# A convolutional feed-forward up-projection: 40 of 44 pairs of feature blocks as seven half-width products each, with activations parked in DRAM until the down-projection

## The chip, the cores and the metric

One NeuronCore of one Trainium2 chip runs the whole layer as one program. The metric is the device time of an execution in microseconds (us). All matmuls take float32r operands; each float32 matrix is split into a rounded part `hi` and a remainder `lo`, and a product is three matmuls (hi·hi, hi·lo, lo·hi).

## The reference

One encoder layer on 512 positions of width 2048: latent attention beside a gated convolution, an output projection, and then the part that the change touches:

```python
h = rmsnorm(x, ffn_norm_g[l])
u = conv3_centred(h @ w_ffn_up[l], ffn_conv_w[l]) + ffn_conv_b[l]   # (512, 2*5632)
g, val = u[..., :D_FF], u[..., D_FF:]
x = x + (jax.nn.silu(g) * val) @ w_ffn_down[l]                       # 5632 -> 2048
return rmsnorm(x, final_norm_g)
```

## The kernel before

Everything is kept transposed: a tile is 128 features (partitions) by 512 positions. Weights come from DRAM as units of 128x1024 (eight 128x128 blocks, 512 KB, array `wall`). For each unit SP issues the load into a `raw` tile (3 buffers), ScalarE casts it to `hi` (line 214), VectorE subtracts to get `lo` (line 211), and TensorE runs 24 matmuls of 512 columns on it (lines 224 and 227 to 231). `hi` and `lo` have two buffers, so the split of a unit can begin when TensorE has finished the unit two before.

`items` is the list of TensorE's work, one entry per unit. `run` walks it: it keeps two units split ahead and three loaded ahead, and calls each item's follow-up functions (`posts`) a given number of items later. A scheduler then sets each engine's final order by its own model of time; each engine runs its queue strictly in order.

A **block** below is one value of `f` (0 to 43): 128 gate features and the 128 value features that belong to them. `up(f)` makes four units of it (two per side, 16 blocks of the contraction over 2048): 96 matmuls of 512 columns. `conv` multiplies the sum in PSUM by the norm factor `rx.r` on VectorE, applies the middle tap and bias on ScalarE (line 465), the two outer taps on VectorE (lines 466 and 467), and silu on the gate side (line 761). `gate` multiplies the sides and splits the result into the pair `acts[f]`, which stays in SBUF. `down(c, f0)` follows after a chunk of eight blocks: 16 units that read the eight pairs and add into the residual tiles `xr` (line 211, `l<-ps,l`). Up and down work therefore alternate by chunk. The last chunk of four goes through `last_half` in two halves of 256 positions (matmuls of 256 columns), followed by the final norm and the stores.

`h2` holds the 16 scaled and split residual tiles, the moving operand of every up-projection matmul. PSUM has eight banks of 128x512.

Of the kernel before, what the change touches and what calls it, by code (L numbers as in the profile page):

```python
# [32 lines left out]
P = 128  # L34
# [17 lines left out]
NT = 76  # L52
# [43 lines left out]
def pack_weights(w_in, w_q_b, w_kv_b, w_o, w_up, w_down):  # L96
# [12 lines left out]
    for i, u in enumerate(UNITS):  # L109
# [24 lines left out]
        elif k == "up":  # L134
            c = u[1] * FF + u[2] * P
            wall[i] = kblock(w_up, 8 * u[3], 8, slice(c, c + P))
# [9 lines left out]
class Item:  # L146
# [3 lines left out]
    def __init__(self, pe, key=None, part=slice(0, UW), posts=()):  # L150
        self.pe, self.key, self.part, self.posts = pe, key, part, list(posts)
# [3 lines left out]
def encoder_block(ctx: ExitStack, tc: tile.TileContext, gx, wall, vecs, rot, out):  # L155
# [3 lines left out]
    lp = ctx.enter_context(tc.tile_pool(name="lp", bufs=KD))  # L159
    xp = ctx.enter_context(tc.tile_pool(name="xp", bufs=2))  # L160
# [14 lines left out]
    def ltile():  # L175

        return lp.tile([P, T], F32, tag="l", name="l")
# [11 lines left out]
    vec = cpool.tile([P, NVEC], F32, name="vec")  # L189
    cs = []  # L190
# [6 lines left out]
    def tables():  # L197
        nc.sync.dma_start(vec, vecs)
        for i in range(2):
            cs.append(ztile())  # L200
            nc.sync.dma_start(cs[i], rot[:, i, :])
# [63 lines left out]
    def run(items, between):  # L265


        todo = [i for i, it in enumerate(items) if it.key is not None]
# [3 lines left out]
        def load():  # L272
            nonlocal loaded
            if loaded < len(todo):
                it = items[todo[loaded]]
                raws.append(load_unit(it.key, it.part))
                for f in between.get(loaded, ()):
                    f()
                loaded += 1
# [3 lines left out]
        for i, it in enumerate(items):  # L283
            while raws and len(ready) < 2:
                j = todo[nsplit]
                ready[j] = split_unit(items[j].key, items[j].part, raws.pop(0))
                nsplit += 1
                load()
# [183 lines left out]
    def proj16(keys, act, posts):  # L472
# [3 lines left out]
        def pe(j):  # L476
            def f(w):
                if j == 0:
                    hold["ps"] = ptile()
                for k in range(8):  # L480
                    mm3(hold["ps"], w, slice(k * P, (k + 1) * P), act[8 * j + k], j == 0 and k == 0, j == 1 and k == 7)
# [241 lines left out]
    for n in range(KD):  # L723
        def post(ps, n=n):
            x, t = xp.tile([P, T], F32, tag="x", name="x"), ztile()
# [10 lines left out]
    for n in range(KD):  # L736
        def post(ps, n=n):
# [5 lines left out]
            split_scaled(h2[n], xr[n], col("ffn_g", n))  # L743

# [3 lines left out]
    acts = {}  # L748

    def up(f):  # L750
        us = [None, None]
        for s in range(2):
            c = s * NF + f

            def conv(ps, s=s, c=c):
                t, u = ztile(), ztile()
                tt(t, ps, rx.r, ALU.mult)
                conv3(u, t, [col("ff_w", i * 2 * NF + c) for i in range(3)], col("ff_b", c))
                us[s] = u
                if s == 0:  # L760
                    nc.scalar.activation(u, u, AF.Silu)  # L761

            def gate(ps, f=f):
                tt(us[1], us[0], us[1], ALU.mult)
                acts[f] = pair()
                split(acts[f], us[1])

            lag = 5 if (f, s) == (0, 0) else 1
            items.extend(proj16([("up", s, f, j) for j in range(2)], h2, [(lag, conv)] + [(lag + 1, gate)] * s))
            if (f, s) == (0, 0):  # L770
                stats_sums(rx)
            if (f, s) == (0, 1):
                items.insert(len(items) - 1, Item(rx.spread, posts=[(1, rx.take)]))

    def down(c, f0):
        for n in range(KD):
            proj8(("down", c, n), lambda: [acts[f0 + k] for k in range(8)],
                  [(1, lambda ps, n=n: tt(xr[n], ps, xr[n], ALU.add))])
# [3 lines left out]
    for c, w in enumerate(CHUNKS):  # L782
        for f in range(starts[c], starts[c] + w):
            up(f)
            if c and f == (starts[c] if c < last else NF - 1):
                down(c - 1, starts[c - 1])
# [12 lines left out]
    HT = T // 2  # L799
# [83 lines left out]
```

## Time and profile before

| | |
|---|---|
| median of 3 runs | 2166.28 us (2164.52 to 2167.59) |
| the profiled execution | 2164.06 us, span 2162.3 us |
| TensorE busy | 2146.0 us, 9648 matmuls |
| VectorE busy | 1101.2 us |
| ScalarE busy | 697.8 us |
| GpSimd busy | 107.0 us, all of it in the first fifth |
| DMA | 211.46 MB, mean 98 GB/s |
| mean granted TensorE clock | 0.997 of 2.4 GHz |

The span is the time from the first to the last instruction; the execution's time holds 1.8 us more. Matmuls overlap, so the mean duration of one (some 390 ns) is no pace; the pace is read from the number of starts in a stretch. A line number is often that of a helper (`tt` is line 211, `mm` is line 224), so the tile names tell what an instruction is.

### The profile page before, as it was taken

What the parts mean: (1) busy time and instruction counts of PE and PEld (TensorE: products, weight loads), DVE (VectorE), ACT (ScalarE), POOL (GpSimd) and SP (SyncE); (2) the same over time, 40 slices, a digit from 0 to 9 for tenths busy, and PEclk for the clock granted to TensorE, in tenths of its full rate; (3) what the DMA queues carried; (4) which work ended last, traced back from release to release, by engine and by line L of the source; (5) the groups of instructions that cost most, each with busy time, mean ns of one, the idle gap of its engine ahead of it and who ended that gap; (6) DMA issues with size and microseconds to landing.
All of it is one profiled execution on the core that took longest, in us unless ns stands there. A gap on an engine that the chain in (4) does not pass through costs nothing.

```text
span 2162.3 us, 23494 instructions
## 1 busy us (share of the span) xinstructions
PE 2146.0 (99%) x9648; PEld 1770.9 (82%) x9648; DVE 1101.2 (51%) x1324; ACT 697.8 (32%) x902; POOL 107.0 (5%) x62
## 2 busy tenths in 40 slices
PE   9999999999999999999999999999999999999997
PEld 7888888888888888888888888888888888888887
DVE  6376787654566444434444344443444434444446
ACT  5253454332234333212332123321333223333324
POOL 4002322300000000000000000000000000000000
PEclk9999999999999999999999999999999999999999
DMA  5322122223533233222333222322222333222322
GB/s 209 98 83 74 64 92 69 78 88 112 145 100 94 95 98 98 92 94 97 97 98 98 96 91 97 97 98 98 96 92 96 98 98 98 97 93 94 126 98 78
DMA packets 63931, 211.46 MB, mean 98 GB/s; under 512 B 6864, under 2 KB 11088, under 8 KB 63824
## 3 DMA queue, kind: packets, MB, share of 16 engines
q1 hardware_dynamic: 63824, 209.97, 29.9%
q8 instruction: 75, 1.23, 0.2%
q14 instruction: 32, 0.26, 0.0%
HBM read 205.75 MB, written 4.19 MB: 97 GB/s over the span
## 4 chain that ended last, share of the span: by engine, by line
PE 95%; DVE 2%; issue 1%; ACT 1%; POOL 1%; DMA 0%; DVEq 0%; ACTq 0%; POOLq 0%
PE ps L224 95%; DVE t L211 1%; DVE lo L211 1%; POOL t L630 0%; ACT t L619 0%; POOL t L211 0%; DVE t L220 0%; ACT hi L214 0%; DMA first<-gx 0%; DVE l L211 0%; ACT t L321 0%; ACT t L219 0%; DVE t L466 0%; ACT t L569 0%; DVEq L878 0%
## 5 line engine op out<-in xcount | busy, mean ns | idle before, releaser
L224 PE MATMUL ps<-t,hi 128*128 128x512 f32 x5808 | 1803.8, 393 | 0.5 <-ACT hi L214 0.5
L224 PEld LDWEIGHTS ps<-t,hi 128*128 128x128 f32 x5808 | 1092.5, 188 | 234.5 <-issue 2.6
L224 PE MATMUL ps<-t,lo 128*128 128x512 f32 x2912 | 1135.7, 392 | 3.0 <-DVE lo L211 3.0
L214 ACT CAST hi<-raw 128x1024 fp32r<-128x1024 f32 (+1 forms) x370 | 386.3, 1044 | 1024.4 <-PE ps L224 953.5
L224 PEld LDWEIGHTS ps<-t,lo 128*128 128x128 f32 x2912 | 547.6, 188 | 131.6 <-DVE lo L211 5.6
L211 DVE TENSOR_TENSOR lo<-raw,hi 128x1024 fp32r<-128x1024 f32 (+1 forms) x369 | 458.1, 1241 | 282.5 <-ACT hi L214 276.9
L211 DVE TENSOR_TENSOR t<-ps,t 128x512 f32<-128x512 f32 (+2 forms) x229 | 154.4, 687 | 395.0 <-PE ps L224 382.4
L211 DVE TENSOR_TENSOR l<-ps,l 128x512 f32<-128x512 f32 (+1 forms) x112 | 68.7, 615 | 250.9 <-PE ps L224 249.1
L211 DVE TENSOR_TENSOR t<-t 128x512 f32<-128x512 f32 (+3 forms) x228 | 159.9, 713 | 47.2 <-ACT t L214 29.9
L224 PE MATMUL ps<-t 128*128 128x256 f32 (+1 forms) x640 | 108.1, 326 | 0.0
L224 PEld LDWEIGHTS ps<-t 128*128 128x128 f32 x640 | 94.6, 190 | 10.4
L214 ACT CAST t<-t 128x512 fp32r<-128x512 f32 (+1 forms) x77 | 46.5, 617 | 120.0 <-DVE t L211 117.7
L467 DVE SCALAR_TENSOR_TENSOR t<-t,vec 128x511 f32<-128x511 f32 x96 | 72.1, 751 | 3.3
L466 DVE SCALAR_TENSOR_TENSOR t<-t,vec 128x511 f32<-128x511 f32 x96 | 71.5, 745 | 2.3 <-ACT t L465 2.3
L465 ACT ACTIVATE t<-t,vec 128x512 f32<-128x512 f32 x88 | 71.6, 814 | 0.8 <-DVE t L211 0.8
L211 POOL TENSOR_TENSOR t<-t 128x512 f32<-128x512 f32 x39 | 65.4, 1678 | 67.1 <-DVE t L211 54.5
L321 ACT ACTIVATE t<-l 128x512 f32<-128x512 f32 (+1 forms) x72 | 39.1, 545 | 58.7 <-DVE l L211 58.6
L761 ACT ACTIVATE t<-t 128x512 f32<-128x512 f32 x44 | 27.8, 632 | 89.8 <-DVE t L467 89.7
L645 DVE RECIPROCAL t<-t 128x512 f32<-128x512 f32 x8 | 26.8, 3353 | 35.8 <-POOL t L630 35.8
L630 POOL PARTITION_ALL_REDUCE t<-t x8 | 26.0, 3248 | 47.0 <-issue 29.7
L619 ACT ACTIVATE t<-t 128x512 f32<-128x512 f32 x32 | 19.6, 631 | 19.7 <-DVE t L211 19.6
L220 DVE SCALAR_TENSOR_TENSOR t<-l,vec,t 128x512 fp32r<-128x512 f32 x32 | 23.5, 746 | 3.1 <-ACT t L219 3.1
(61 smaller groups left out, 351.8 us busy)
## 6 DMA issues: line engine op xcount, KB each, us to landing
raw<-wall SPq DMA_DIRECT2D x372, 512.0 KB, 3.5
x<-gx SPq DMA_DIRECT2D x16, 256.0 KB, 3.5
out<-t SPq DMA_DIRECT2D x16, 256.0 KB, 3.2
l<-gx SPq DMA_DIRECT2D x15, 256.0 KB, 6.6
raw<-wall SPq DMA_DIRECT2D x6, 256.0 KB, 3.0
t<-rot SPq DMA_DIRECT2D x2, 256.0 KB, 4.1
first<-gx SPq DMA_DIRECT2D x1, 264.0 KB, 3.3
vec<-vecs SPq DMA_DIRECT2D x1, 216.0 KB, 5.9
```

The costliest lines, as they stand in the source:

```text
L211: (eng or nc.vector).tensor_tensor(out=o, in0=a, in1=b, op=op)
L214: nc.scalar.copy(out=dst[0], in_=src)
L220: nc.vector.scalar_tensor_tensor(out=dst[1], in0=src, scalar=g, in1=dst[0].bitcast(F32), op0=ALU.mult, op1=ALU.subtract)
L224: nc.tensor.matmul(ps, lhsT=w, rhs=x, start=start, stop=stop)
L321: nc.scalar.activation(sq, src, AF.Square)
L465: nc.scalar.activation(o, p, AF.Identity, bias=bias, scale=w[1])
L466: nc.vector.scalar_tensor_tensor(out=o[:, 1:], in0=p[:, :T - 1], scalar=w[0], in1=o[:, 1:], op0=ALU.mult, op1=ALU.add)
L467: nc.vector.scalar_tensor_tensor(out=o[:, :T - 1], in0=p[:, 1:], scalar=w[2], in1=o[:, :T - 1], op0=ALU.mult, op1=ALU.add)
L619: nc.scalar.activation(e, e, AF.Exp, scale=SCALE)
L630: nc.gpsimd.partition_all_reduce(pr[hd, TB], z["e"][0], P, bass_isa.ReduceOp.add)
L645: nc.vector.reciprocal(ri, pr[hd, TB])
L761: nc.scalar.activation(u, u, AF.Silu)
```

## The change

Four blocks (f = 0 to 3) stay plain. For the other 40, the gate and value sides with the even and odd blocks of the contraction form a 2x2 arrangement of weights (`a11`, `a12` gate, `a21`, `a22` value), and the two halves of the 512 positions with even and odd feature tiles form a 2x2 arrangement of activations. Seven products in Winograd's form of Strassen's scheme take the place of eight: per block 7 items of 24 matmuls of 256 columns, 168 in all. The units of `up` are packed anew (even and odd blocks of the contraction).

- `make_operands(i)`, eight calls between the plain units, reads two residual tiles back from DRAM, scales them by gain and `rx.r`, makes the activation sums and splits them.
- `seven` makes the weight sums: three 128x1024 additions on VectorE (`s`), and a fourth (`a21` plus `a22`) by a DMA that adds into SBUF, issued from GpSimd. All seven operands are then split as before. Sums in PSUM are seeded, kept and added by ScalarE copies and two VectorE additions of 256 columns; `rx.r` is no longer applied there.
- `save` writes `xr` and each `acts` pair to DRAM from GpSimd's queue; `restore` reads them through SP's queue. The five chunks of `down` follow in a row after the last block.
- `raw` has 8 buffers (3 before), `hi`/`lo` 3 each (2 before); loads of a block run further ahead; the tiles `l` and `x` now come out of the common pool `tp` (80 tiles; before 76 and 18 apart). A small table `nvec` of negated taps is made by VectorE once `vec` has landed.

```diff
-NT = 76
+NT = 80
+NPLAIN = 4
+AHEAD = 4
...
-    wraw = ctx.enter_context(tc.tile_pool(name="wraw", bufs=3))
-    wsp = ctx.enter_context(tc.tile_pool(name="wsp", bufs=2))
+    wraw = ctx.enter_context(tc.tile_pool(name="wraw", bufs=8))
+    wsp = ctx.enter_context(tc.tile_pool(name="wsp", bufs=3))
...
-            while raws and len(ready) < 2:
+            while raws and len(ready) < (3 if items[todo[nsplit]].source else 2):
...
-                load()
+                while loaded < min(len(todo), nsplit + (AHEAD if items[todo[min(loaded, len(todo) - 1)]].source else 3)):
+                    load()
...
+    def save(name, src):
+        saved[name] = [(dram.tile([P, T], F32, name=f"{name[0]}{name[1]}_{i}"), t.dtype) for i, t in enumerate(src)]
+        for (o, _), t in zip(saved[name], src):
+            nc.gpsimd.dma_start(o, t.bitcast(F32))
...
+    def make_operands(i):
+        (a,), (b,) = restore(("xr", 2 * i)), restore(("xr", 2 * i + 1))
+        for k, t in ((2 * i, a), (2 * i + 1, b)):
+            nc.vector.scalar_tensor_tensor(out=t, in0=t, scalar=col("ffn_g", k), in1=rx.r, op0=ALU.mult, op1=ALU.mult)
+        u, v = ztile(), ztile()
+        tt(half(u, 0), half(a, 0), half(a, 1), ALU.subtract)
+        tt(half(u, 1), half(b, 1), half(a, 1), ALU.subtract)
+        nc.vector.scalar_tensor_tensor(out=half(v, 0), in0=half(a, 0), scalar=-1.0, in1=half(u, 1), op0=ALU.mult, op1=ALU.subtract)
+        nc.vector.scalar_tensor_tensor(out=half(v, 1), in0=half(v, 0), scalar=-1.0, in1=half(b, 0), op0=ALU.mult, op1=ALU.subtract)
+        one = tile_r()
+        split((half(one, 0), half(one, 1)), half(a, 0))
+        got = {1: (half(one, 0), half(one, 1))}
+        for src, names in ((u, (5, 7)), (v, (6, 4)), (b, (2, 3))):
+            p = pair()
+            split(p, src)
...
+    def product(ps, w, q, start):
+        n = len(operands)
+        for k in range(n):
+            for i, (a, b) in enumerate(((0, 0), (0, 1), (1, 0))):
+                nc.tensor.matmul(ps, lhsT=w[a][:, k * P:(k + 1) * P], rhs=operands[k][q][b], start=start and k == 0 and i == 0,
+                                 stop=k == n - 1 and i == 2, skip_group_check=True)
...
+        def first():
+            raw["s"] = wraw.tile([P, UW], F32, tag="raw", name="raw")
+            tt(raw["s"], raw["a11"], raw["a21"], ALU.add)
+            nc.gpsimd.dma_start(raw["a21"], wall[UIDX[units["a22"]]], accum_op=ALU.add)
+            return parts(raw["a11"])
...
+        order = (("f", 1, True, load("a11", "a21"), first, [(1, seed)]),
+                 ("g", 7, True, load("a22"), lambda: parts(raw["s"]), [(1, keep("s7", "g"))]),
+                 ("h", 6, False, load("a12"), plus("a22"), [(1, keep("u2", "h"))]),
+                 ("f", 2, False, load(), lambda: parts(raw["a12"]), [(1, call("c11", "f"))]),
+                 ("h", 5, False, load(), lambda: parts(raw["a21"]), [(1, call("c22", "h", "s7"))]),
+                 ("g", 4, False, load(), lambda: parts(raw["a22"]), [(1, call("c21", "g", "u2"))]),
+                 ("h", 3, False, load(), plus("a12"), [(1, call("c12", "h"))]))
...
+    for i in range(KD // 2):
+        plain[(6, 7, 8, 9, 10, 14, 15, 16)[i]].posts.append((0, lambda i=i: make_operands(i)))
+    items.extend(plain)
+    for f in range(NPLAIN, NF):
+        items.extend(up_seven(f))
...
+    at = len(items) - 7
+    items[at].posts.append((0, lambda: fetch(range(0, 2))))
+    items[at + 4].posts.append((0, lambda: fetch(range(2, 6))))
...
+    for c in range(last):
+        at = len(items)
+        down(c)
+        for f in range(CHUNKS[c + 1]):
+            items[at + f].posts.append((0, lambda f=f, c=c: fetch([starts[c + 1] + f])))
```

In the rows of the programs that follow, `lo_...<-raw_...` is a weight split, `raw<-raw` a weight sum, `t_5364` (before) the norm factor, and the seven items of a block are called products 0 to 6.

VectorE, one block in the middle of the up-projection, before:

```order
L211 TENSOR_TENSOR t_10511<-ps_10445,t_5364 128x512
L211 TENSOR_TENSOR lo_10506<-raw_10407,hi_10505 128x1024
L466 SCALAR_TENSOR_TENSOR t_10512<-t_10511,vec_87,t_10512 128x511
L467 SCALAR_TENSOR_TENSOR t_10512<-t_10511,vec_87,t_10512 128x511
L211 TENSOR_TENSOR lo_10544<-raw_10437,hi_10543 128x1024
L211 TENSOR_TENSOR t_10579<-ps_10518,t_5364 128x512
L211 TENSOR_TENSOR lo_10574<-raw_10474,hi_10573 128x1024
```

The same place after the change, from the split of product 1's weights to that of product 4's:

```order
L229 TENSOR_TENSOR lo_8214<-raw_8180,hi_8213 128x1024
L486 SCALAR_TENSOR_TENSOR t_8218<-t_8187,nvec_84,t_8218 128x511
L229 TENSOR_TENSOR raw_8180<-raw_8180,raw_8089 128x1024
L487 SCALAR_TENSOR_TENSOR t_8218<-t_8187,nvec_84,t_8218 128x511
L486 SCALAR_TENSOR_TENSOR t_8252<-t_8154,vec_83,t_8252 128x511
L229 TENSOR_TENSOR lo_8248<-raw_8180,hi_8247 128x1024
L487 SCALAR_TENSOR_TENSOR t_8252<-t_8154,vec_83,t_8252 128x511
L229 TENSOR_TENSOR lo_8283<-raw_8121,hi_8282 128x1024
L229 TENSOR_TENSOR raw_8180<-raw_8180,raw_8121 128x1024
L229 TENSOR_TENSOR t_8218<-t_8252,t_8218 128x512
L229 TENSOR_TENSOR lo_8326<-raw_8048,hi_8325 128x1024
```

Weight sums now stand between the splits, and the taps of the block before and the product of its two sides stand between the splits of products 1 to 4.

ScalarE, the same stretch, before:

```order
L214 CAST hi_9573<-raw_9475 128x1024
L465 ACTIVATE t_9580<-t_9579,vec_87 128x512
L761 ACTIVATE t_9580<-t_9580 128x512
L214 CAST hi_9611<-raw_9505 128x1024
L214 CAST hi_9641<-raw_9542 128x1024
L465 ACTIVATE t_9648<-t_9647,vec_87 128x512
L214 CAST t_9685<-t_9648 128x512
```

And after the change, from silu on; the two copies at line 905 keep sums out of PSUM (products 1 and 2), and line 925 is the first quarter of the result:

```order
L794 ACTIVATE t_8012<-t_8012 128x512
L232 CAST hi_8085<-raw_7808 128x1024
L232 CAST t_8051<-t_7978 128x512
L232 CAST hi_8117<-raw_7849 128x1024
L905 COPY t_8091<-ps_8060 128x256
L905 COPY t_8123<-ps_6038 128x256
L232 CAST hi_8150<-raw_7940 128x1024
L925 COPY t_8154<-ps_8017 128x256
```

The copies, on whose second one product 4 waits, now stand behind the split of the block's finished activations.

VectorE at the seam between plain units and the first seven-product block, before (there two plain blocks follow each other):

```order
L211 TENSOR_TENSOR lo_5391<-raw_5285,hi_5390 128x1024
L466 SCALAR_TENSOR_TENSOR t_5404<-t_5403,vec_87,t_5404 128x511
L467 SCALAR_TENSOR_TENSOR t_5404<-t_5403,vec_87,t_5404 128x511
L211 TENSOR_TENSOR t_5404<-t_5397,t_5404 128x512
L211 TENSOR_TENSOR t_5442<-t_5404,t_5441 128x512
L211 TENSOR_TENSOR lo_5435<-raw_5315,hi_5434 128x1024
```

And after, the first 12 of the 24 rows from the split of product 2's weights up to that of product 3's (calls 6 and 7 of `make_operands`, and the end of the last two plain blocks):

```order
L229 TENSOR_TENSOR lo_6088<-raw_5974,hi_6087 128x1024
L826 SCALAR_TENSOR_TENSOR t_5945<-t_5945,vec_83,t_5394 128x512
L229 TENSOR_TENSOR t_5949<-t_5943 128x256
L229 TENSOR_TENSOR raw_5974<-raw_5974,raw_5910 128x1024
L229 TENSOR_TENSOR t_5949<-t_5945,t_5943 128x256
L830 SCALAR_TENSOR_TENSOR t_5950<-t_5943,t_5949 128x256
L229 TENSOR_TENSOR t_5955<-t_5943,t_5955 128x256
L831 SCALAR_TENSOR_TENSOR t_5950<-t_5950,t_5945 128x256
L229 TENSOR_TENSOR t_5959<-t_5949,t_5958 128x512
L229 TENSOR_TENSOR t_5963<-t_5950,t_5962 128x512
L229 TENSOR_TENSOR t_5967<-t_5945,t_5966 128x512
L813 SCALAR_TENSOR_TENSOR t_5981<-ps_5758,t_5394 128x512
```

Where one split followed another after at most four short instructions, the splits of products 2 and 3 have 23 instructions between them. In SP's queue at the start of the program, units 1, 2 and 3 now stand ahead of the second tile of `x`; before, that tile stood ahead of unit 1.

## Rows read from the trace of the kernel before

**Rows 1.** Page, parts 1 and 2: busy time, then granted clock in 40 slices.

```profile
PE 2146.0 (99%) x9648; PEld 1770.9 (82%) x9648; DVE 1101.2 (51%) x1324; ACT 697.8 (32%) x902; POOL 107.0 (5%) x62
...
PEclk9999999999999999999999999999999999999999
```

**Rows 2.** Chain of waits in order of time: start, us, what.

```profile
353.55 1795.13 PE ps L224 x8058
```

**Rows 3.** Stretches: us, busy us and (starts) by engine, clock, DMA share, GB/s.

```profile
10.00:15.00 5.00, 5.00 (x23) 4.09 (x23) 3.08 (x5) 5.00 (x8) 2.48 (x3) 1.00 1.04 399
...
1288.00:1900.00 612.00, 612.00 (x2676) 502.34 (x2675) 270.96 (x304) 171.79 (x192) 0.00 (x0) 1.00 0.29 96
```

**Rows 4.** Timeline of TensorE: first of 48 matmuls of 256 columns, next group.

```profile
314.28 0.40 PE L224 MATMUL ps<-hi,t 128*128 128x256 f32 x2
...
319.93 0.63 PE L224 MATMUL ps<-t,hi 128*128 128x512 f32 x2
```

**Rows 5.** Timeline of VectorE in the last chunk, one eviction per 12 matmuls.

```profile
2105.64 0.42 DVE L211 TENSOR_TENSOR l<-ps,l 128x256 f32<-128x256 f32 x1
...
2112.84 0.42 DVE L211 TENSOR_TENSOR l<-ps,l 128x256 f32<-128x256 f32 x1
```

**Rows 6.** VectorE by line and shape: count, busy us, mean ns, idle before.

```profile
L211 DVE TENSOR_TENSOR lo<-raw,hi 128x1024 fp32r<-128x1024 f32 x363 | 452.4, 1246 | 280.5 <-ACT hi L214 275.0 <-PE ps L224 5.3
...
L211 DVE TENSOR_TENSOR t<-t 128x512 f32<-128x512 f32 x111 | 75.1, 686 | 6.5 <-ACT t L321 4.5 <-ACT t L365 0.2
L467 DVE SCALAR_TENSOR_TENSOR t<-t,vec 128x511 f32<-128x511 f32 x96 | 72.1, 751 | 3.3
...
L211 DVE TENSOR_TENSOR t<-t 128x512 fp32r<-128x512 f32 x76 | 64.4, 864 | 29.6 <-ACT t L214 29.6
...
L220 DVE SCALAR_TENSOR_TENSOR t<-l,vec,t 128x512 fp32r<-128x512 f32 x32 | 23.5, 746 | 3.1 <-ACT t L219 3.1
L220 DVE SCALAR_TENSOR_TENSOR t<-l,first,t 128x512 fp32r<-128x512 f32 x15 | 21.0, 1438 | 1.7 <-ACT t L219 1.7
...
L211 DVE TENSOR_TENSOR l<-ps,l 128x256 f32<-128x256 f32 x32 | 13.4, 423 | 5.8 <-PE ps L224 4.0
```

**Rows 7.** ScalarE by line and shape.

```profile
L214 ACT CAST hi<-raw 128x1024 fp32r<-128x1024 f32 x363 | 382.0, 1052 | 1014.4 <-PE ps L224 946.7 <-issue 64.9 <-ACT t L608 0.9
L465 ACT ACTIVATE t<-t,vec 128x512 f32<-128x512 f32 x88 | 71.6, 814 | 0.8 <-DVE t L211 0.8
L214 ACT CAST t<-t 128x512 fp32r<-128x512 f32 x76 | 45.8, 617 | 117.7 <-DVE t L211 117.7
L761 ACT ACTIVATE t<-t 128x512 f32<-128x512 f32 x44 | 27.8, 632 | 89.8 <-DVE t L467 89.7
...
L365 ACT COPY t<-ps 128x256 f32<-128x256 f32 x1 | 0.4, 353 | 0.0
```

**Rows 8.** Timeline of VectorE in a plain block.

```profile
1003.53 1.23 DVE L211 TENSOR_TENSOR lo<-raw,hi 128x1024 fp32r<-128x1024 f32 x1 [0.17 <-ACT hi L214]
1004.67 0.74 DVE L466 SCALAR_TENSOR_TENSOR t<-t,vec 128x511 f32<-128x511 f32 x1
1005.45 0.75 DVE L467 SCALAR_TENSOR_TENSOR t<-t,vec 128x511 f32<-128x511 f32 x1
```

**Rows 9.** Page, part 6: DMA issues, KB each, median us to landing.

```profile
raw<-wall SPq DMA_DIRECT2D x372, 512.0 KB, 3.5
```

**Rows 10.** Timelines of ScalarE and VectorE at the start: second `x` tile, last split.

```profile
8.70 0.72 ACT L219 ACTIVATE t<-l,first 128x512 fp32r<-128x512 f32 x1 [0.72 <-DMA l<-gx]
...
41.90 1.22 DVE L211 TENSOR_TENSOR lo<-raw,hi 128x1024 fp32r<-128x1024 f32 x1
```

**Rows 11.** GpSimd by line and shape.

```profile
L211 POOL TENSOR_TENSOR t<-t 128x512 f32<-128x512 f32 x39 | 65.4, 1678 | 67.1 <-DVE t L211 54.5 <-ACT t L214 7.8 <-ACT t L321 2.4
```

More of the change, by code (lines that the diff above doesn't have):

```diff
@@ L743, in post @@
             split_scaled(h2[n], xr[n], col("ffn_g", n))
+            save(("xr", n), [xr[n]])
         proj8(("oc", n), lambda: yl, [(1, post)])
[L748 to L773 removed]
@@ new lines, in restore, with conv_up @@
+    def restore(name):
+        ts = [tp.tile([P, T], dt, tag="t", name="t") for _, dt in saved[name]]
+        for o, (d, _) in zip(ts, saved[name]):
+            nc.sync.dma_start(o.bitcast(F32), d)
+        return ts
+    def conv_up(u, t, s, f):
+        c = s * NF + f
+        taps = [nvec[:, i * NF + f:i * NF + f + 1] for i in range(3)] if s else [col("ff_w", i * 2 * NF + c) for i in range(3)]
+        conv3(u, t, taps, col("ff_b", c))
+        if s == 0:
+            nc.scalar.activation(u, u, AF.Silu)
@@ new lines, in encoder_block @@
+    operands = []
+    def make_operands(i):
[13 more added lines that the diff above has]
+            split(p, src)
+            for j, q in enumerate(names):
+                got[q] = half(p[0], j), half(p[1], j)
+        operands.append(got)
@@ new lines, in up_seven, with c11, c22, c21 @@
+    def up_seven(f):
+        tg, tv, us = [], [], [None, None]
+        def c11(ps):
+            tg.append(ztile())
+            nc.scalar.copy(out=half(tg[0], 0), in_=ps)
+        def c22(ps, other):
+            tv.append(ztile())
+            tt(half(tv[0], 1), ps, other, ALU.add)
+        def c21(ps, other):
+            tt(half(tv[0], 0), ps, other, ALU.add)
+            us[1] = ztile()
+            conv_up(us[1], tv[0], 1, f)
+        def c12(ps):
+            nc.scalar.copy(out=half(tg[0], 1), in_=ps)
+            us[0] = ztile()
+            conv_up(us[0], tg[0], 0, f)
+        units = {f"a{s + 1}{j + 1}": ("up", s, f, j) for s in range(2) for j in range(2)}
+        its = seven(f, units, {"c11": c11, "c22": c22, "c21": c21, "c12": c12})
+        its[-1].posts.append((2, lambda: gated(us, f)))
+        return its
@@ L780, in encoder_block @@
     starts = [sum(CHUNKS[:i]) for i in range(len(CHUNKS))]
     last = len(CHUNKS) - 1
[L782 to L786, printed above, removed]
+    plain = []
+    for f in range(0, NPLAIN - 2):
+        plain += [it for its in up_plain(f, False) for it in its]
+    four = [it for f in range(NPLAIN - 2, NPLAIN) for it in up_plain(f, True)]
@@ new lines, in encoder_block, with fetch @@
+    plain += [its[j] for j in range(2) for its in four]
+    plain.insert(2, Item(rx.sums, posts=[(1, rx.chain)]))
+    plain.insert(4, Item(rx.spread, posts=[(1, rx.take)]))
+    for i in range(KD // 2):
+        plain[(6, 7, 8, 9, 10, 14, 15, 16)[i]].posts.append((0, lambda i=i: make_operands(i)))
+    plain[-2].posts.append((0, mark))
+    items.extend(plain)
+    for f in range(NPLAIN, NF):
+        items.extend(up_seven(f))
+    acts = {}
+    def fetch(fs):
+        for f in fs:
+            acts[f] = restore(("act", f))
```

107 lines of the change are left out of this document (90 added, 17 removed).

## The prediction

> **What bounds the kernel now.** I read the busy shares first [rows 1]: TensorE is busy 99% of the span at the full clock (2.4 GHz) in every slice, VectorE 51%. Then the chain of waits [rows 2]: from 353.55 us on, one unbroken piece of TensorE work of 1795 us is what ends last. So only TensorE's own time counts there, until something else becomes later. Its pace comes from starts per stretch [rows 3]: 612.00 / 2676 = 0.2287 us for each matmul of 512 columns. For 256 columns there are two places with fresh weights in every matmul: 48 from 314.28 to 319.93 [rows 4] are 0.1177 us each; in the last chunk five evictions later [rows 5], (2112.84 - 2105.64) / 60 = 0.120 us. So half the width costs 51.5 to 52.5% of the full one; I take 0.119.
>
> **The gain.** A block costs 96 x 0.2287 = 21.96 us now and 168 x 0.119 = 19.99 us after, if TensorE alone sets the pace. 1.97 us x 40 = 78.7 us. With 0.1177 it is 87, with 0.120 it is 72.
>
> The Trainium skill's page "TensorE: Matmul & The Clock Gate", section "Back-to-back issue gap", gives 518 cycles for 512 columns and 262 for 256, about 216 and 109 ns; the gain would by that be an estimated 95 us. The rows show 228.7 and 118 to 120, more than both, and I go by the rows.
>
> **Can VectorE feed it?** Per block after: 7 splits and 3 weight sums of 128x1024 at 1.246, 2 additions of 256 columns at 0.423, 4 outer taps at 0.75, the product of the sides at 0.686 and one split at 0.69 to 0.86 [rows 6]: 12.46 + 0.85 + 3.0 + 0.69 + 0.8 = 17.8 us against 20.0. (The sums are not in the trace; they have the shape and engine of the split, and I take its time.) Now it is 4 splits and some 5.8 us, 10.8 against 22.0. Back to back the starts lie closer than the durations: 1003.53 to 1004.67 is 1.14 for a split [rows 8]. ScalarE has 7 casts at 1.052, 2 middle taps at 0.814, silu, one cast at 0.617 and 5 copies at about 0.36 [rows 7], 12 us. Neither is over the limit, but VectorE at 89% leaves little for waits, so I followed the one loop that closes over the engines.
>
> With three `hi`/`lo` buffers, product 1's weights can be cast when product 5 of the block before has ended. From there, in the order shown: cast 1.05; on VectorE split, tap, sum, tap, tap, split, tap, split, sum, product of the sides = 5 x 1.246 + 4 x 0.75 + 0.69 = 9.9; on ScalarE the cast of that product 0.62, the cast for product 5 1.05, two copies 0.71. Sum 13.3, some 12.8 at back-to-back starts, and I allow 0.5 for hand-overs. The second copy reads the bank that product 4 adds to, so product 4 waits for it. Product 4 should start five products after the loop's beginning: 5 x 2.856 = 14.3. Slack about 1 us. So I cost the steady part at nothing, with the end that 0.5 us a block is lost (20 us).
>
> **The seam into the seven-product part.** This is the largest loss I see. A call of `make_operands` is on VectorE 2 scalings at 0.746, 4 half operations at some 0.43, a half split and 3 splits at about 0.69: some 5.7 us, eight times. The last two calls, the ends of the last two plain blocks, a weight sum and the splits are in a row behind the split of product 2. That split cannot be over before about 3 us after the first product begins, as its buffer comes free only with the last plain unit. From there to the split for product 6, that one included, stand 35 instructions: 6 of 1024 columns at 1.246 (7.5), 19 of 511 or 512 at some 0.715 (13.6) and 10 of 256 at some 0.43 (4.3): 25 us by durations, 23 by starts. Product 6 then starts at 26 to 28 us and not at 6 x 2.856 = 17.1. A loss of 9 to 11, and some 2 more in the next block, whose evictions come late too: 12 us, bounds 5 and 20. Nothing covers it, as every product needs all eight operands.
>
> **The start.** The second tile of `x` lands at 8.70 [rows 10]. In the new queue three units of 0.52 MB are ahead of it and only the two halves of the first before; at 399 GB/s [rows 3] that is 4 us. VectorE then still works off the splits of `x` until 41.90 [rows 10], so most of it stays: +4 us, bounds 0 and 8. One small VectorE instruction there waits for `vec`, which lands at about the same time; the third buffer may give a little back. The attention part I take at no change, 3 us either way.
>
> **The seam into the down-projection.** SP issues 68 restores of 0.26 MB and 12 units up to the thirteenth unit of the first chunk: 24 MB, 60 us at 399 GB/s, and from the release of the first tiles to the need it has some 80. The first eight pairs, four residual tiles and three units (6.8 MB, 17 us) end about when the last block does: +2 us, bounds 0 and 6. The down-projection itself keeps 24 x 0.2287 per unit; VectorE has one split and one addition per 5.5 us there.
>
> **Off the path.** Saves: 3 DMA issues per block on GpSimd, which stands idle there; they wait for finished activations, and only the adding DMA behind them has a reader soon. It goes out after the first weight sum of its block and must land before the cast for product 4, about 15 us later. A plain unit lands in 3.5 us [rows 9]. No row shows a DMA that adds or one issued by GpSimd: nearest below is 3.5 us, above I have nothing but the 15 us from which it costs. I take it as hidden.
>
> **Sum.** 2164.06 - 78.7 + 12 + 4 + 2 = 2103.4 against the profiled execution's own 2164.06. The median of the runs lies 2.2 us above that one, so 2105.6, rounded 2106.
>
> **The rivals.**
> 1. Slower: GpSimd's work slows VectorE until VectorE sets the pace. For it: while GpSimd added tiles of 1678 ns each [rows 11], scalings on VectorE took 1438 ns and not 746, and the small splits average 864 over a stretch that it partly shares, where 690 is usual [rows 6]. With a factor of 864 / 686 = 1.26 on everything a block takes 22.3 us, 40 x 0.35 = 14 over the present, and with 15 + 4 + 2 for seams and start about 2201. It decides from a factor of about 1.21 on (21.5 us a block). Against: GpSimd does no arithmetic there, it only issues. The Trainium skill's "SBUF — State Buffer", section "Who interferes with whom", says that an operation of VectorE with two inputs in SBUF collides only with GpSimd reading SBUF, and infers that writing descriptors is not that; by it this rival would cost 0, and no row here shows GpSimd issuing. 8%.
> 2. The loop slips: hand-overs cost 1.5 to 2 us and not 0.5, product 4 waits 0.5 to 1 us in each block, 20 to 40 us in all: 2126 to 2146. For it: a dozen hand-overs and a slack of 1 us. 17%.
> 3. The adding DMA takes over 15 us and product 4 waits in each block; at 16 us 2146, at 17 no gain is left. For it: 2.6 MB of weights and 0.5 MB of saves a block share the engines, and addition reads what it writes. Against: 0.3 of the engines' time is used now, 0.5 then. 5%, over half of it slower.
> 4. Half the width costs exactly half: 168 x 0.1144 = 19.2 us, a gain of 110, 2075. Both places in the trace speak against it. The skill's section cited above points this way with a ratio of 0.506. 4%.
> 5. The scheme does not do what it says, since the extra matmuls, seams and waits eat the gain to within 0.2%: 3%.
>
> **How the numbers follow.** The forecast (pace of TensorE, seams as above, 2086 to 2125) has 63%. Its lower end is 0.1177 with small seams: 2166.3 - 87 + 5 + 0 + 2; its upper one 0.120 with the larger ones: 2166.3 - 72 + 20 + 8 + 3. The range takes in rival 2: 2086 to 2147, leaving out rivals 1, 3, 4 and 5, 2 in 10. Faster by over 0.2% (about what a measurement of this kernel can tell from no change): 63 + 17 + 4 + 2 = 86%. Same: 3%. Slower: 8 + 3 = 11%.
>
> **What would show it.** In the profile after: 20.0 us between equal events of neighbouring blocks, matmuls of 256 columns at 0.118 to 0.120, and a granted clock of full speed throughout. VectorE near 17.8 us a block with splits still at 1.25. One gap of TensorE of some 12 us in all around the first seven-product block, waiting for VectorE. Little waiting where the down-projection begins. I am wrong if blocks take over 20.5 us: then the releaser in front of product 4 tells which rival it is, VectorE and ScalarE (2), splits longer than 1.25 (1), or a DMA (3).

## The result, and the profile after

The changed kernel takes 2096.4 us (median of four executions, 2095.5 to 2097.0), the kernel before 2165.5 in the same series: ratio 0.968, interval 0.966 to 0.970. The forecast was 2106 in a range of 2086 to 2147. The profiled execution took 2095.81 us with a span of 2094.0, against 2164.06 and 2162.3. Of the runs below, one execution of e1 took 2554 us at a granted clock of 0.749 and is left out of e1's numbers.

The page after, parts 1, 2 and 6 (busy time, granted clock in 40 slices, and two rows of the DMA issues: KB each, median us to landing); it answers to [rows 1, 9]:

```profile
PE 2064.5 (99%) x12530; PEld 1845.7 (88%) x12530; DVE 1374.0 (66%) x1645; ACT 900.1 (43%) x1254; POOL 200.2 (10%) x206
...
PEclk9999999999999998999999999999999999999999
...
act<-t POOLq DMA_DIRECT2D x88, 256.0 KB, 5.4
...
raw<-wall POOLq DMA_DIRECT2D x40, 512.0 KB, 6.9
```

TensorE has 2882 matmuls more and is busy 81.5 us less; its clock dips in one slice. The DMA that adds lands in 6.9 us. Then the long piece of the chain of waits (start, us, what), as [rows 2]:

```profile
810.56 780.06 PE ps L854 x6600
1590.62 0.47 PE ps L242 x2
1591.09 2.83 PE ps L854 x24
1593.91 486.42 PE ps L242 x2312
```

From 810.56 us to the end of the last seven-product block there is only TensorE work, 780 us without a wait, and the down-projection goes on in the same way for another 486. Stretches of the changed kernel (us, busy us and starts by engine in the order PE, PEld, DVE, ACT, POOL, then clock, DMA share, GB/s), as [rows 3]:

```profile
700.00:780.00 80.00, 80.00 (x355) 65.46 (x354) 61.24 (x99) 34.37 (x50) 3.11 (x5) 1.00 0.47 157
780.00:822.00 42.00, 28.00 (x177) 25.93 (x176) 32.06 (x48) 18.10 (x29) 3.07 (x5) 0.76 0.26 78
...
1590.00:1700.00 110.00, 110.00 (x497) 90.83 (x496) 43.50 (x48) 24.87 (x26) 1.09 (x2) 1.00 0.87 324
...
900.00:1500.00 600.00, 600.00 (x5096) 600.00 (x5095) 496.06 (x549) 351.43 (x486) 60.13 (x90) 1.00 0.52 159
```

The pace of the blocks is read from ScalarE's last copy of each (duration, then first and last start):

```profile
L937 ACT COPY t<-ps x40: 366/376/377, 821.8 to 1594.8; 128x256 f32<-128x256 f32 x40
```

(1594.8 - 821.8) / 39 = 19.82 us a block, 0.1180 a matmul. The one place in these 40 blocks where TensorE waits is the first of them. Timeline of TensorE there, its first matmul and those with a wait ahead of them (start, duration, idle before and what ended it):

```profile
780.85 0.40 PE L854 MATMUL ps<-t,hi 128*128 128x256 f32 x2
...
786.94 0.39 PE L854 MATMUL ps<-t,hi 128*128 128x256 f32 x1 [1.57 <-DVE t L229]
...
787.88 0.38 PE L854 MATMUL ps<-t,hi 128*128 128x256 f32 x1 [0.32 <-DVE t L229]
...
793.38 0.58 PE L854 MATMUL ps<-t,hi 128*128 128x256 f32 x1 [4.92 <-ACT t L232]
795.67 0.58 PE L854 MATMUL ps<-t,hi 128*128 128x256 f32 x1 [1.71 <-DVE t L229]
...
797.88 0.79 PE L854 MATMUL ps<-t,hi 128*128 128x256 f32 x2 [0.47 <-ACT ps L900]
...
810.56 0.80 PE L854 MATMUL ps<-t,hi 128*128 128x256 f32 x2 [5.00 <-ACT t L905]
```

From 780.85 to 821.8 this block takes 41.0 us and not 19.8: a **loss of 21.1 us**. The waits sum to 14.0. The first two and the fourth are for operands of the activations (VectorE's subtraction), the third for a cast of them, all four in products 0 and 1; the fifth, 0.47 us, is for the copy that seeds product 2's sum, the last for the two copies that product 4 needs. The rest, 7 us, is mostly the clock: 0.76 over the stretch, 0.50 (the lower of the two levels, 1.2 GHz) between 790 and 800, within and behind the long wait. Some 48 matmuls start 0.213 us after one another and not 0.118, some 4.5 to 5 us in all.

VectorE's split for product 6, and what ScalarE does in front of product 4 (the cast of the last plain block's activations, then the two copies):

```profile
806.91 1.22 DVE L229 TENSOR_TENSOR lo<-raw,hi 128x1024 fp32r<-128x1024 f32 x1
```

```profile
809.61 0.62 ACT L232 CAST t<-t 128x512 fp32r<-128x512 f32 x1 [1.90 <-DVE t L229]
810.14 0.64 ACT L905 COPY t<-ps 128x256 f32<-128x256 f32 x2
```

### The profile page after: what moved, and what is told of

Same layout as the page of the kernel before. It is cut to its first block, busy times and chain, and to the rows that moved or that the text cites. A ratio compares the mean times of both kernels' runs of the same rounds, so it can differ in the third digit from the quotient of the medians.

```text
span 2094.0 us, 30792 instructions
## 1 busy us (share of the span) xinstructions
PE 2064.5 (99%) x12530; PEld 1845.7 (88%) x12530; DVE 1374.0 (66%) x1645; ACT 900.1 (43%) x1254; POOL 200.2 (10%) x206
## 4 chain that ended last, share of the span: by engine, by line
PE 61%; DVE 1%; issue 0%; ACT 0%; DVEq 0%; ACTq 0%
PE ps L854 37%; PE ps L242 23%; DVE t L229 0%; DVE lo L229 0%; ACT hi L232 0%; DVE t L487 0%; ACT t L232 0%; DVE t L486 0%; DVEq L1078 0%; ACT t L347 0%; ACT t L905 0%; ACT st L369 0%; DVE st L370 0%; DVE st L372 0%; DVE st L374 0%
## 5 line engine op out<-in xcount | busy, mean ns | idle before, releaser
L242 PE MATMUL ps<-t,hi 128*128 128x512 f32 x3248 | 1010.2, 393 | 2.6 <-ACT t L237 2.0
L232 ACT CAST hi<-raw 128x1024 fp32r<-128x1024 f32 (+1 forms) x490 | 511.7, 1044 | 845.2 <-PE ps L242 517.0
L854 PE MATMUL ps<-t,hi 128*128 128x256 f32 x4480 | 791.9, 281 | 14.0 <-ACT t L905 5.0
L242 PEld LDWEIGHTS ps<-t,hi 128*128 128x128 f32 x3248 | 610.5, 188 | 140.2 <-ACT t L237 2.9
L229 DVE TENSOR_TENSOR lo<-raw,hi 128x1024 fp32r<-128x1024 f32 (+1 forms) x489 | 602.6, 1233 | 190.6 <-ACT hi L232 180.2
L854 PEld LDWEIGHTS ps<-t,hi 128*128 128x128 f32 x4480 | 682.5, 188 | 16.1 <-ACT t L905 5.2
L242 PE MATMUL ps<-t,lo 128*128 128x512 f32 x1632 | 638.5, 393 | 0.0
L854 PE MATMUL ps<-t,lo 128*128 128x256 f32 x2240 | 614.2, 280 | 0.0
L854 PEld LDWEIGHTS ps<-t,lo 128*128 128x128 f32 x2240 | 417.1, 189 | 0.0
L242 PEld LDWEIGHTS ps<-t,lo 128*128 128x128 f32 x1632 | 307.6, 189 | 66.4 <-issue 0.5
L229 DVE TENSOR_TENSOR t<-t 128x512 f32<-128x512 f32 (+4 forms) x276 | 185.0, 685 | 20.9 <-ACT t L341 11.7
L229 DVE TENSOR_TENSOR raw<-raw 128x1024 f32<-128x1024 f32 x120 | 146.0, 1217 | 0.0
```

The source lines that it names most:

```text
L229: (eng or nc.vector).tensor_tensor(out=o, in0=a, in1=b, op=op)
L232: nc.scalar.copy(out=dst[0], in_=src)
L242: nc.tensor.matmul(ps, lhsT=w, rhs=x, start=start, stop=stop)
L854: nc.tensor.matmul(ps, lhsT=w[a][:, k * P:(k + 1) * P], rhs=operands[k][q][b], start=start and k == 0 and i == 0, stop=k == n - 1 and i == ...
```

## The experiments

My theory at this point: the steady part is TensorE's own pace with a small reserve in the loop that the prediction followed, and everything that went otherwise lies at the seam into the seven-product part. Rivals: the seam is late by the place of the operand calls, by VectorE's amount of work, or by the order of a queue; the reserve is not the loop's but VectorE's throughput; GpSimd does slow VectorE.

### The seam: place, amount, or order

**e1**: three plain blocks interleaved by halves, not two.

```diff
-    for f in range(0, NPLAIN - 2):
+    for f in range(0, NPLAIN - 3):
-    four = [it for f in range(NPLAIN - 2, NPLAIN) ...
+    four = [it for f in range(NPLAIN - 3, NPLAIN) ...
-        plain[(6, 7, 8, 9, 10, 14, 15, 16)[i]].posts...
+        plain[(6, 7, 8, 9, 10, 12, 13, 14)[i]].posts...
```

> The same four plain blocks, but the last three (not two) are interleaved by halves of the contraction, so that the tiles of the even features come free two units earlier and the last three calls of make_operands stand at plain items 12, 13, 14 and not 14, 15, 16. VectorE's work is the same. In the changed kernel TensorE loses 21 us against its own pace between the first matmul of the first seven-product block (780.85) and the end of its product 6 (about 821.8; 19.8 at pace): 14.0 us of waits, the rest at a lower granted clock. Theory A, position: the last calls come too late because their tiles come free too late; two units earlier is 11 us, the loss falls to 10 us or less, 2083 to 2087. Theory B, amount: VectorE was already 87% busy from 720 to 780 us, so moving work only shifts what is late; the loss stays at 16 us or more, 2091 to 2100.

Measured: 2099.1, ratio 0.970 (0.968 to 0.971). The loss is 25.6 us (first matmul 779.23, last copy 824.6). Theory A's number falls. The operand waits shrink as it said, from 8.5 us to 1.0, but the ends of three blocks now crowd the same place, and two other waits, the second above all, take it all back, on TensorE (the first is for VectorE's eviction of a plain block, the second for the copies):

```profile
785.44 0.80 PE L854 MATMUL ps<-t,hi 128*128 128x256 f32 x2 [3.05 <-DVE t L813]
...
812.99 0.80 PE L854 MATMUL ps<-t,hi 128*128 128x256 f32 x2 [11.44 <-ACT t L905]
```

**e2**: six plain blocks.

```diff
-NPLAIN = 4
+NPLAIN = 6
-        plain[(6, 7, 8, 9, 10, 14, 15, 16)[i]].posts...
+        plain[(6, 8, 10, 12, 14, 22, 23, 24)[i]].posts...
```

> Six plain blocks and 38 seven-product blocks; the first five calls of make_operands are spread over plain items 6 to 14, the last three stand in the last four units as before (items 22 to 24 of 26). Two blocks more at 21.96 and not 19.82 cost 4.3 us. Theory A, position: three calls and the ends of two blocks still crowd the last four units, the loss at the seam stays near 21 us, 2098 to 2103. Theory B, amount: VectorE has 44 us more of plain units before the seam, so nothing but the last three calls is left there; the loss falls to 8 us or less, 2085 to 2089.

Measured: 2091.45, ratio 0.966 (0.964 to 0.967); loss 12.7 us (822.84 to 855.3). Nearer to theory B: the operand waits are gone. The two waits that are left on TensorE, the first of them for the copy that seeds a sum (line 900), and the two instructions of ScalarE in front of the second one:

```profile
829.75 0.51 PE L854 MATMUL ps<-t,hi 128*128 128x256 f32 x2 [1.10 <-ACT ps L900]
...
843.62 0.80 PE L854 MATMUL ps<-t,hi 128*128 128x256 f32 x2 [7.94 <-ACT t L905]
```

```profile
840.92 0.63 ACT L794 ACTIVATE t<-t 128x512 f32<-128x512 f32 x1 [2.10 <-DVE t L487]
...
843.20 0.64 ACT L905 COPY t<-ps 128x256 f32<-128x256 f32 x2
```

This one, 7.94 us, neither theory had: ScalarE waits 2.10 us for the taps of the last plain block before silu, and then for the product of its sides; the copies, which need nothing of that block, stand behind it in the queue.

**e5**: the changed kernel with that one follow-up later.

```diff
-... [(lag, conv)] + [(lag + 1, lambda ps: gated(us, f))] * s ...
+... [(lag, conv)] + [(lag + (5 if f == NPLAIN - 1 else 1), lambda ps: gated(us, f))] * s ...
```

> Only the place of one follow-up is changed: the product of the two sides of the last plain block, with the split and the save behind it, is called three products later. In ScalarE's queue the two copies that product 4 of the first seven-product block waits for (5.00 us at 810.56 in the changed kernel) then stand ahead of silu and of the cast of those activations, and not behind them. Theory queue: the wait is made by that order alone; the copies follow the cast at 805.53 and product 4 starts 3 to 4 us earlier, and about 2 us of the lower granted clock behind the gap go too: 2089 to 2093. Theory backlog: VectorE is late with everything at this place, so another of its results (a split) holds TensorE instead: 2095 to 2098.

(It is four items later, not three as written there: 6 in place of 2.)

The profiled execution took 2086.45; the four were 2086.45, 2060.59, 2088.28 and 2061.17 (median 2073.8, ratio 0.955, interval 0.949 to 0.962). In the profiled one the wait is gone, which is theory queue and a little more: the loss is 13.4 us (779.34 to 812.5). TensorE's waits now, those over half a microsecond:

```profile
785.43 0.38 PE L854 MATMUL ps<-t,hi 128*128 128x256 f32 x1 [1.57 <-DVE t L229]
...
791.86 0.58 PE L854 MATMUL ps<-t,hi 128*128 128x256 f32 x1 [4.99 <-ACT t L232]
794.15 0.58 PE L854 MATMUL ps<-t,hi 128*128 128x256 f32 x1 [1.71 <-DVE t L229]
```

**e12**, the same kernel again, since two executions 26 us below the others were not understood.

> The kernel of e5_late_gate once more. Of its four executions two took 2086.5 and 2088.3 and two 2060.6 and 2061.2; the one profiled was of the first kind. Theory A: a second state of this program, 26 us apart, that no record yet shows; several of six executions are near 2061 again, and if the profiled one is, its pace in the seven-product blocks tells whether the 26 us are 6720 matmuls x 0.0038 us. Theory B: a disturbance of that series alone; all lie between 2084 and 2090.

Measured: 2088.2 to 2090.3 in four executions, median 2090.17, ratio 0.965 (0.963 to 0.966). None was near 2061, and no profile shows such an execution: what those two were stays open (their granted clock, 0.993 and 0.994, is that of the others), and I go by the others. By the profile of e12 the loss is 14.5 us (781.26 to 815.6).

**e6**: e2 and e5 together (six plain blocks, the later follow-up).

> Six plain blocks as in e2_six_plain, whose one large wait left is 7.94 us of product 4 on the same two copies, and the later follow-up of e5_late_gate with it. Theory queue: 4 to 5 us of that wait and 2 us at the lower clock go: 2083 to 2087. Theory backlog: 2089 to 2093 as in e2_six_plain.

Measured: 2086.8, ratio 0.963 (0.962 to 0.965), at the upper end of theory queue. The loss is 7.0 us (824.98 to 851.8), with waits of 1.10 and 3.45.

**e11**: the same with five plain blocks, calls at items 6, 8, 10, 11, 12, 18, 19, 20.

> Five plain blocks, 39 seven-product blocks, and the later follow-up of e5_late_gate. One plain block more costs 2.14 us against four, one less gives 2.14 against six. The first seven-product block loses 13.4 us with four plain blocks and the late gate, 7.0 with six. Theory amount: 11 us of VectorE's idle time are enough for the two operand waits that four plain blocks leave (4.99 and 1.71 us, and the lower clock behind them): 2081 to 2085. Theory position (the last three calls come in the last four units, whatever stands ahead): 2087 to 2090.

Measured: 2088.14, ratio 0.964 (0.962 to 0.965). The number is theory position's, the trace is not: the four operand waits of e5 (1.57, 0.33, 4.99 and 1.71) came down to two, of 2.47 and 0.32, but product 4 of the next block waited 1.81 us on the same kind of copies, and the granted clock was 0.83 in 840 to 850. Inconclusive between the two, and a sign that this order has to be looked at in each block near the seam.

So the seam has two causes. The operand waits are VectorE's work too late: less of it ahead of the seam removes them (e2), and so, nearly, does an earlier place (e1). The wait of product 4 is ScalarE's order, shown by the one edit of e5 and again by e6; in e1 it grew to 11.44 us and hid what the place was worth. The places of e1 with the later follow-up of e5 were not run, so place against amount stays open. e6, e11 and e12 are all faster than the changed kernel: 0.963 to 0.965 against 0.968, and the intervals do not touch.

### The reserve of the steady part

**e4** and **e3**: two subtractions a block done twice, of the weights of products 5 and 6, and of products 1 and 2.

```diff
             split((hi, lo), src)
+            if name in TWICE:
+                tt(lo, src, hi.bitcast(F32), ALU.subtract)
```

> The same two extra subtractions of 128x1024 per block, but for the weights of products 5 and 6, in a stretch where VectorE waits four times per block (0.4 to 1.2 us each) and which the loop does not contain. Both theories: VectorE 18.6 us of 19.8, no change, 2094 to 2099. If it is slower by as much as the run with the extra work inside the loop, it is VectorE's amount of work and not the loop that sets the limit.

> In each seven-product block the subtractions that split the weights of products 1 and 2 are done twice on VectorE (the same result is written again): 2 x 1.14 us more in the loop from product 5 of the block before to the copies that product 4 waits for. Theory loop: that loop has a slack of about 1.8 us in the changed kernel (ScalarE stands idle 0.84 us in front of the copies, and product 4 starts 0.9 us after them), so a block gets 0.3 to 1.3 us longer, 12 to 50 us in all: 2108 to 2146. Theory throughput: VectorE is busy 16.3 of 19.8 us a block and 18.6 with this, still under TensorE; no change, 2094 to 2099.

Measured: e4 2123.4 (20.48 us a block), e3 2220.5 (23.05 a block). Both are slower than either theory allowed. What TensorE waits for between 900 and 1500 us is not the loop's copies, and VectorE is busy only 539.39 (e4) and 482.32 (e3) of 600 us:

```profile
PE ps L855 <- DVE lo L230: 12.4, 30, 0.4
```

(e4; in e3 the same releaser has 47.9 us in 42 waits, ScalarE's casts 5.6 us in 14, and the clock is 0.97.) In the order that came out, the second subtraction of a split stands behind the split of the next product, which itself waits until a buffer is free. The edit thus did more than add work: it made a result late by its place in an in-order queue. The pair shows that, and does not measure the reserve.

**e10**: the same amount, but as work that nobody waits for.

```diff
             conv_up(us[1], tv[0], 1, f)
+            e = ztile()
+            for _ in range(4):
+                tt(e, tv[0], tv[0], ALU.mult)
```

> The changed kernel with four products of 128x512 more on VectorE in each seven-product block (2.4 us at back-to-back starts, as much as e3 and e4 added), written to a tile that nobody reads; in VectorE's queue they stand singly between the splits. Theory amount: VectorE is busy 18.7 of 19.8 us a block, no single split is late by more than 0.6 us; no change, 2094 to 2099, and e4_twice_out_of_loop was slower because the second subtraction of a split stood behind another split that waited for its buffer. Theory limit: VectorE's queue has no room for 2.4 us at any place; 0.5 us or more a block as in e4_twice_out_of_loop, 2115 to 2160.

Measured: 2154.3, 58 us slower; a block takes 21.37 us and not 19.82, 1.55 more, though VectorE is busy only 523.57 of 600 us. This time TensorE waits for exactly the copies that close the loop of the prediction, 1.35 us each time:

```profile
PE ps L854 <- ACT t L905: 37.9, 28, 1.6
```

The loop in the changed kernel, VectorE and ScalarE from the cast of product 1's weights to the copies:

```profile
1195.88 1.23 DVE L229 TENSOR_TENSOR lo<-raw,hi 128x1024 fp32r<-128x1024 f32 x1 [0.54 <-ACT hi L232]
...
1204.21 0.69 DVE L229 TENSOR_TENSOR t<-t 128x512 f32<-128x512 f32 x1
```

```profile
1194.80 1.05 ACT L232 CAST hi<-raw 128x1024 fp32r<-128x1024 f32 x1 [1.54 <-PE ps L854]
...
1204.93 0.62 ACT L232 CAST t<-t 128x512 fp32r<-128x512 f32 x1 [0.60 <-DVE t L229]
1206.39 1.05 ACT L232 CAST hi<-raw 128x1024 fp32r<-128x1024 f32 x1 [0.84 <-PE ps L854]
1207.35 0.64 ACT L905 COPY t<-ps 128x256 f32<-128x256 f32 x2
```

And in e10:

```profile
1202.69 1.22 DVE L229 TENSOR_TENSOR lo<-raw,hi 128x1024 fp32r<-128x1024 f32 x1
...
1213.95 0.68 DVE L229 TENSOR_TENSOR t<-t 128x512 f32<-128x512 f32 x1
```

```profile
1216.81 0.78 PE L854 MATMUL ps<-t,hi 128*128 128x256 f32 x4 [1.34 <-ACT t L905]
```

From the split of product 1's weights to the product of the sides it was 8.33 us and is 11.26. The 2.93 between them are three of the four multiplications (0.60 each at back-to-back starts) and one split (1.14) that the new order put ahead of the product. Without the 0.84 us that ScalarE waits for a buffer, the loop in the changed kernel lasts 1194.80 to 1207.99 less 0.84 = 12.35 us, and five products last 14.16: a reserve of 1.8 us. e10 put 2.9 into it, 1.1 too much; the wait is 1.35 and the block 1.55 longer, so the hand-overs at both ends, which the subtraction leaves out, take 0.2 to 0.4 of the reserve. Theory limit holds, but as the loop's limit, since 2.4 us would have fitted into VectorE's idle time. No run put the same work outside the loop without making a result late, so that half is argued from the wait alone.

**e8**: two `hi`/`lo` buffers as before.

```diff
-    wsp = ctx.enter_context(tc.tile_pool(name="wsp", bufs=3))
+    wsp = ctx.enter_context(tc.tile_pool(name="wsp", bufs=2))
-            while raws and len(ready) < (3 if items[todo[nsplit]].source else 2):
+            while raws and len(ready) < (2 if items[todo[nsplit]].source else 2):
```

> Two hi/lo buffers as in the kernel before, not three. Up to the up-projection this undoes the one edit that I suspect of the gain there: the changed kernel reaches the spread of rx 2.1 us earlier (710.38 and 712.51). Theory buffer: it is back at 712 to 714. Theory elsewhere (norm tables, pools): it stays at 710 to 711. In the seven-product blocks a split can then start only when the product two before has ended, and cast, subtraction and hand-overs need 2.7 of the 2.83 us of a product, with other work of VectorE in front: each product waits 0.3 to 1 us, 2.1 to 7 us a block, 2180 to 2380 in all. If the third buffer is not needed there: 2094 to 2100.

Measured: 2140.1; 20.72 us a block (TensorE waits for a split once in each, 0.6 us), so the third buffer is worth 0.90 us a block, less than I feared. At the start and at the end of the first part TensorE has these matmuls of a norm each, timeline of TensorE (e8, then the changed kernel, then the kernel before):

```profile
56.50 1.02 PE L242 MATMUL ps<-t,ones 128*128 128x512 f32 x2
...
714.44 1.02 PE L242 MATMUL ps<-t,ones 128*128 128x512 f32 x2
```

```profile
53.99 1.02 PE L242 MATMUL ps<-t,ones 128*128 128x512 f32 x2
...
710.38 1.02 PE L242 MATMUL ps<-t,ones 128*128 128x512 f32 x2
```

```profile
53.19 1.02 PE L224 MATMUL ps<-t,ones 128*128 128x512 f32 x2
...
712.51 1.02 PE L224 MATMUL ps<-t,ones 128*128 128x512 f32 x2
```

Theory buffer holds, and a little more: 714.44 is past its 714. With two buffers the start is 3.3 us later than before; with three it is not told apart from before, since the first norm comes at 52.05 to 54.15 us in the eleven traces (the changed kernel, e1 to e7, e10 to e12) whose edits all come later. Between the two norms it was 659.3 us before, is 657.9 with two buffers and 656.4 with three (ten of those eleven agree within 0.1 us, e12 is 0.6 longer). So of the 2.9 us the third buffer explains 1.5; what made the other 1.4 was not tried.

### GpSimd, and half the width by itself

**e7**: an addition on GpSimd for the adding DMA.

```diff
-            nc.gpsimd.dma_start(raw["a21"], wall[UIDX[units["a22"]]], accum_op=ALU.add)
...
+                tt(raw["a21"], raw["a21"], raw["a22"], ALU.add, nc.gpsimd)
```

> The fourth weight sum is made by an addition of 128x1024 on GpSimd, not by the adding DMA: arithmetic in place of issuing. By the trace of the kernel before (1678 ns for 128x512 on GpSimd) it takes about 3.4 us a block. Theory collision (rival 1 of the prediction, with its mechanism put in on purpose): VectorE's instructions beside it take up to twice as long (1438 for 746 there), VectorE is late by 1 to 2 us in each block, 2136 to 2176. Theory no collision: the sum is ready earlier than by the DMA (6.9 us), VectorE's splits stay at 1.24, 2094 to 2099.

Measured: 2097.6, the same as the changed kernel. Both theories are half right. Lines of VectorE and GpSimd between 900 and 1500 us (count, busy us, mean ns), first e7, then the changed kernel:

```profile
L229 DVE TENSOR_TENSOR lo<-raw,hi 128x1024 fp32r<-128x1024 f32 x213 | 288.6, 1355 | 66.7 <-ACT hi L232 66.7
...
L229 POOL TENSOR_TENSOR raw<-raw 128x1024 f32<-128x1024 f32 x30 | 115.8, 3859 | 24.1 <-DVE raw L229 24.1
```

```profile
L229 DVE TENSOR_TENSOR lo<-raw,hi 128x1024 fp32r<-128x1024 f32 x213 | 260.0, 1221 | 67.9 <-ACT hi L232 67.9
...
L877 POOL DMA_DIRECT2D raw<-wall x30 | 26.9, 898 | 32.3 <-DVE raw L229 32.3
```

GpSimd's arithmetic does lengthen VectorE's splits, by 0.134 us on the mean of seven, 0.95 us a block; but that lies inside the reserve, and TensorE does not wait once. GpSimd issuing DMAs leaves them at 1221; in the kernel before, with GpSimd idle in that stretch, they are at 1226.

**e9**: the kernel before, each matmul of `proj16` as two of 256 columns.

```diff
-                    mm3(hold["ps"], w, slice(k * P, (k + 1) * P), act[8 * j + k], ...)
+                    for e in range(2):
+                        for i, (a, b) in enumerate(((0, 0), (0, 1), (1, 0))):
+                            nc.tensor.matmul(hold["ps"][:, e * 256:(e + 1) * 256], ...,
+                                             rhs=act[8 * j + k][b][:, e * 256:(e + 1) * 256], ...)
```

> The kernel before, with each of the 96 up-projection matmuls of 512 columns of a block made as two of 256 columns (the same weights, 192 a block, 44 blocks); nothing else is changed. It costs the half width by itself. Theory A: 0.118 us each as in the seven-product blocks (19.82 / 168): 22.66 and not 21.96 us a block, 0.70 x 44 = 31 us, 2197. Theory B: half the width costs half (0.1144), and the 0.118 comes from something else in the seven-product blocks: no change, 2163 to 2169.

Measured: 2200.9 against 2165.9. It is theory A. That it is 4 us more than I said comes from 48 units of the first part, which use the same function and which I had left out: between the two norms e9 takes 668.1 us (53.08 to 721.14) and not 659.3. Of the 38.4 us between the spans that leaves 29.7 for the up-projection, against the 31 expected. The chain over a stretch of up-projection alone:

```profile
722.17 186.56 PE ps L483 x1584
```

186.56 / 1584 = 0.1178 us, where half of 0.2287 is 0.1144. The extra price of half the width belongs to the width and not to the scheme.

## Why the prediction was right, step by step

The spans differ by 68.3 us. By the terms of the sum, forecast and then measured:

| term | forecast | measured | from |
|---|---|---|---|
| pace, 40 blocks | -78.7 | -85.6 | 40 x (21.96 - 19.82) |
| seam into the seven-product part | +12 | +21.1 | 780.85 to 821.8 |
| start | +4 | +0.8 | 53.99 against 53.19 |
| attention part | 0 | -2.9 | 656.4 against 659.3 |
| loop, steady part | 0 | 0 | no wait in 780 us |
| down-projection and rest | +2 | -1.7 | remainder |

- **Pace.** The step was right, its value a little off: I took 0.119 between 0.1177 [rows 4] and 0.120 [rows 5]; it is 0.1180, and e9 has 0.1178 with nothing else changed. That also decides against rival 4. The row read on TensorE itself was the better one, the row read by evictions the worse. By the Trainium skill ("TensorE: Matmul & The Clock Gate", "Back-to-back issue gap", its cycles for an isolated matmul) it would have been an estimated 0.109; the measurement decides against it.
- **The loop** was the right one, and costing it at nothing was right: 12.35 us against the 13.3 I had, a reserve of 1.4 to 1.8 and not 1. e10 shows it close when 2.9 us are put in, at just the copies in front of product 4. Rival 2 would have needed over 1.4 us more of hand-overs in each block.
- **The seam** was rightly named as the largest loss and mis-sized by 9 us, over the upper bound of 20. The count of VectorE's instructions held: the split for product 6, forecast for 26 to 28 us after the first matmul, was over 27.3 us after it (808.13). But I had TensorE wait there, and it never did. It had waited 8.5 us in products 0 and 1 already, for the operands of the last calls, which stand in the same row of VectorE's instructions and which I had put in the count but not in TensorE's path. Two more things were missing. The ends of the last plain block hold ScalarE's queue, so product 4 waits for the copies (5.00 us; e5 removes it) and starts only at 810.56, when the split for product 6 is long done. And I had assumed the full clock throughout; within and behind the two waits of 5 us TensorE ran at the lower level, which cost some 5 us.
- **The start.** The changed queue makes the second tile of `x` late as I said, if less so: ScalarE takes it up at 11.56 us and not at 8.70 [rows 10], 2.9 us of the forecast 4. In e8 (12.20 us) this ends as a loss of 3.3 us. The third buffer, which I had give back "a little", gives back all that can be told: the +0.8 of the table lies within the spread of equal programs (52.05 to 54.15 us). The third buffer also explains 1.5 of the 2.9 us by which the attention part, which I had put at no change, is shorter.
- **Down-projection.** No wait at its start or in the 486 us that follow: TensorE is busy 110 of 110 us while the DMAs run at 0.87 and 324 GB/s.
- **VectorE** takes 496.06 / 600 x 19.82 = 16.4 us a block (17.8 forecast; back-to-back starts lie closer than durations, as noted there), ScalarE 11.6 (12).
- **Rivals 1 and 3.** GpSimd issues 0.9 us per adding DMA and VectorE's splits stay at 1.22 us; with arithmetic on GpSimd they grow to 1.36 (e7). That agrees with the Trainium skill, "SBUF — State Buffer", section "Who interferes with whom", by which a VectorE instruction with two inputs in SBUF contends with a GpSimd instruction that reads SBUF. The adding DMA lands in 6.9 us, against the 15 from which it costs.

The errors of the seam (+9) and of the pace (-7) nearly cancel, which is luck; the start, the attention part and the down-projection with the rest, together 10 us better than I said, are why the profiled execution came out 8 us under its sum of 2103.4; the median lies 0.6 above it and not 2.2.

## What to carry to other kernels

When a new stage follows an old one, list for each in-order queue what of the old stage's end stands ahead of what the new stage needs first: here one follow-up, called four items later, gave back a third of the seam. Follow TensorE's path through such a row from the first product on, and not only at the last instruction of the count. Cost a gap of TensorE at more than its length, as the clock behind it may be lower. And a reserve is that of a loop, not of an engine's idle time: VectorE had 3.4 us free per block, the loop some 1.4 to 1.8, and 2.9 us put into the loop cost 1.55 us a block.

## What the runs showed of the hardware that I had not expected

- Within and behind waits of 5 us TensorE's granted clock was at the lower level (0.50 in 790 to 800; three matmuls of 256 columns per 0.64 us, against 0.354 later). After a shorter wait it fell only when TensorE was at work again: in e6 (3.45 us, over at 841.26) it was 1.00 up to 842 and 0.50 in 843 to 844, in e11 (1.81 us, over at 842.04) 1.00 up to 843 and 0.50 in 844 to 846. In e10, with a wait of 1.35 us in each block, it stayed at 1.00.
- Matmuls of 256 columns take 0.1178 to 0.1180 us, 3% more than half of 512 columns. While they run, weight loads fill the time (600 of 600 us, against 502 of 612 in [rows 3]); whether these set the pace was not tried.
- A GpSimd addition of 128x1024 takes 3.86 us and lengthens the VectorE splits beside it; issuing a DMA from GpSimd (0.56 to 0.90 us) does not.
